# VectorE in the written order during part 1, and a longer lag for one head's first scores

## The chip, the cores and the metric

The kernel runs on one core of a Trainium2 chip. A core has five engines, each with its own instruction stream: TensorE (PE, matmuls), VectorE (DVE), ScalarE (ACT), GpSimd (POOL), and SyncE (SP), which issues most of the DMA transfers. The metric is the device time of one launch in microseconds, as the median of several runs. One launch runs one step of the whole layer.

## The reference

One layer of a streaming speech encoder, with 2048 prompt frames and 64 frames of a second stream ("sample") with a cache of 256 keys. Everything is float32. Cut to what matters here:

```python
h = rms_norm(x, norm1_g) * (1 + sc1) + sh1            # sc1, sh1, ... from silu(c) @ w_ada
z = h @ w_in
glu_a, glu_b, q, k, v, g_conv, g_attn = split(z)

u = glu_a * sigmoid(glu_b)                            # convolution branch, 512 channels
y = silu(layer_norm(depthwise_conv(u, width=31) + b)) @ w_conv_out

q, k = rms_norm(q), rms_norm(k)                       # attention branch, 8 heads of 64
s = q @ k.T * scale + rel_bias[head, clip(q_pos - k_pos)]
o = softmax(mask(s)) @ v                              # own chunk of 64 frames and the 8 before
attn_out = o @ w_attn_out

x = x + gt1 * ((sigmoid(g_conv) * y + sigmoid(g_attn) * attn_out) @ w_o)
gate, up = split((rms_norm(x, norm2_g) * (1 + sc2) + sh2) @ w_ffn_in)
x = x + gt2 * ((silu(gate) * up) @ w_ffn_out)
```

## The kernel before

To keep float32 accuracy at TensorE's faster rate, each operand is split into a high part and a low remainder (`hh` and `hl` for the input, `whi` and `wlo` for a weight, `ph` and `pl` for attention weights, `part_h` and `part_l` for what is stored). A product is three matmuls: high by high, low by high, high by low.

Part 1 makes everything up to the two branches' results. It takes the frames in four blocks (`PBLOCKS`, 576 rows and then three times 512), numbered 0 to 3. For each block the list `ORDER` names stages: the projections `q`, `k`, `v`, the four channel tiles of the convolution input, and the gates `g`. After a block's `v` its eight heads of attention are started; they run beside the block's convolution and gates and the next block's projections. In block 0 prompt heads alternate with the sample's heads, so the order of heads is (0,0), ("s",0), (0,1), ... ("s",7), then (1,0), (1,1) and so on. Part 2 reads the stored results back (`cin` is such a tile), merges the branches and runs the feed-forward part.

The code does not emit one step after the other. A planner (class `Stream`) counts the estimated load of each engine while instructions are written out. Work beside the projections is held in generators, sorted into lanes (`Lane`): norms, heads, convolution taps, the tail of the convolution. Every 500 ns of counted TensorE load a lane may advance by one step, if its due time has come and if VectorE or ScalarE isn't counted too full. A due time is the counted end of what the step needs, plus a constant. So the written order is already a schedule by the planner's count, not by the chip.

The instruction order on an engine is then made by a scheduler that may re-sort what was written; `tc.manual_schedule(engines=...)` turns that off for the engines listed, which then issue as written. In the kernel before this holds in part 1, after the first block's start (`first_block`), for TensorE alone (line 1642) until `ordered.close()`. VectorE, ScalarE, GpSimd and SyncE are re-sorted.

What a head does, in `attend` (from line 1509): `fetch` loads `q`, `kk` and a bias tile; after the due time in `loaded` the four score matmul groups (`sc`) follow one another, each as soon as VectorE has taken the row maximum (`pr`, `sm`) of one before it. ScalarE takes the exponent, VectorE the reciprocal of the sum. Then the weights are transposed (`ptp`), split into `ph` (ScalarE) and `pl` (VectorE) and multiplied by `vv` into `po`. `finish_head` divides, splits and stores the result (`o_p`, `part_h`, `part_l`).

The other names in the rows: `y<-u,wd,y` is one tap of the depthwise convolution on VectorE, `kn<-kn,r` a key or query norm that uses `r` from GpSimd, `ssq` and `t` its sums. `conv_norm` (from line 1294) is the tail of the convolution: normalise, then for each of four channel tiles a `y` and a `ln` step on VectorE, a split into `part_h` (ScalarE) and `part_l` (VectorE, `part_l<-ln`) and a store to `c_d`. The two tiles of `parts()` have `NS` = 2 buffers each, shared with all stores of part 1. `wmod` are weights of the modulation (`w_ada`), multiplied into `pa`. All compute instructions go through one helper, `Meter.run`, so nearly all rows of the profile carry its line, L105.

Of the kernel before, what the change touches and what calls it, by code (L numbers as in the profile page):

```python
# [622 lines left out]
def streaming_layer(ctx: ExitStack, tc: tile.TileContext, I, O):  # L623
# [481 lines left out]
    def cached_kv():  # L1105
        rows_ = [(src, j) for j in range(CACHE // P) for src in (ck, cv)]
        ts = []
        for i, (src, j) in enumerate(rows_):
            for src_, j_ in rows_[len(ts) : i + 2]:
                t = temp("cache")  # L1110
                nc.sync.dma_start(t, src_[j_ * P : (j_ + 1) * P])
                ts.append((t, stream.load["pe"] + CACHE_LAG))
            t, landed = ts[i]
            yield landed
            if src is ck:
                store_kq(t, P, k_d, j * P)
            else:
                store_v(t, P, j * P)
            yield
# [349 lines left out]
    def load_bias(h):  # L1469
        for r in (0, HD):  # L1470
            nc.sync.dma_start(
                bias[r : r + HD, HD - r : 640 - r],
                bass.AP(tensor=rb_d.tensor, offset=rb_d.offset + 768 * h + HD, ap=[[1, HD], [1, 576]]),
            )
        return bias

    ahead_qk, spare = {}, {"open": False, "heads": []}
    order, loaded, now = [], {}, {"scored": -1, "finished": -1, "bias": None}
# [8 lines left out]
    def fetch_qk(i):  # L1487
        if i < len(order) and ("qk", i) not in now:
            x, h = order[i]
            if spare["open"]:  # L1490
                spare["heads"].append(i)
            now["qk", i] = load_qk(x, h, *spans(x))

    def fetch(i):
        if i < len(order) and i not in loaded:
            x, h = order[i]
            fetch_qk(i)
            if now["bias"] is None or now["bias"][0] != h:
                now["bias"] = h, load_bias(h)
            first = x != "s" and (not i or order[i - 1][0] not in (x, "s"))  # L1500
            lag = FIRST_LAG if first else QK_LAG
            loaded[i] = max(stream.load["pe"] + BIAS_LAG, ahead_qk.get(i, stream.load["pe"] + lag))

# [5 lines left out]
    def attend(i):  # L1509
        x, h = order[i]  # L1510
        q0, nq, k0, nk = spans(x)
        yield lambda: now["scored"] == i - 1
        fetch(i)
        fetch_v(i)
        if not i:
# [7 lines left out]
        for t in range(0, nq, P):  # L1523
            n = min(P, nq - t)
            if x not in (0, "s"):
                ps = ps_a.tile([P, 2, 512], F32, tag="s", name="sc")
                for j in range(2):
                    for d in range(2):
                        pe.matmul(ps[:, j, :320], q2[:, d, t : t + P], kk[:, t + 320 * j : t + 320 * j + 320], start=d == 0, stop=d == 1)
                w, src, bs = 640, ps[:, :, :320], bias[:, ::-1]  # L1530
            else:
                w = nk if x == "s" else t + P

                if "banks" not in now:
                    sc = ps_a.tile([P, 2, 512], F32, tag="s", name="sc")
                    now["banks"] = [sc[:, 0:1], sc[:, 1:2]]
                ps = now["banks"].pop(0)
                now["banks"].append(ps)
                for d in range(2):
                    pe.matmul(ps[:n, 0, :w], q2[:, d, t : t + n], kk[:, :w], start=d == 0, stop=d == 1)  # L1540
                src, bs = ps[:n, 0:1, :w], bias[:n, 64:384][:, ::-1] if x == "s" else bias[:, :w][:, ::-1]
            pr, sm, free, ready = softmax_max(src, n, w, bs)
            tiles.append((pr, sm, n, w))
            if t + P < nq:
                yield free + PE_LAG, SCORE_ROOM
            else:
                fetch(i + 1)
                if (x, order[min(i + 2, len(order) - 1)][0]) in ((0, 0), ("s", "s")):
                    fetch_qk(i + 2)
                now["scored"] = i  # L1550
            if t:
                softmax_scale(*tiles[-2], x in ON_ACT)
# [86 lines left out]
    W = Weights((nc.sync, act, dve, gps), wpool, dram, stream, list(weight_order()), source, 3, 5, lambda key: key[0] in KEPT)  # L1639
    first_block(xs)  # L1640
    ordered = ExitStack()
    ordered.enter_context(tc.manual_schedule(engines={mybir.EngineType.PE}))
    norm_lane.add(cached_kv())
    mods = mod_steps()
    norms = {}
# [734 lines left out]
```

## Time and profile before

| | |
|---|---|
| median of 3 runs | 2958.93 us (2955.85 to 2965.5) |
| the profiled execution | 2957.35 us |
| its span in the trace | 2955.5 us |
| granted TensorE clock, mean | 0.995 |
| TensorE busy | 2892.0 us |
| VectorE busy | 2049.8 us |
| ScalarE busy | 1364.3 us |
| GpSimd busy | 1161.4 us |

The span is what the trace covers from the first to the last instruction; the time of the run has 1.85 us around it. A busy share is an average over the whole launch and says little about one stage, so the text reads rows of the stretch in question. In a row of the timeline the first two numbers are start and duration, and a bracket at the end gives the idle time of that engine just before it and what ended it. PEclk is the granted clock as a share of full speed.

### The profile page before, as it was taken

To read this page: it belongs to the slowest core of one execution; us is meant where nothing else is said; L and a number is where in the kernel's file an instruction comes from. 1 tells how busy PE (TensorE), PEld (TensorE's weight loads), DVE (VectorE), ACT (ScalarE), POOL (GpSimd) and SP (SyncE) were. 2 spreads that over 40 slices of the span, in tenths; PEclk is the share of its full clock that TensorE was granted. 3 is DMA by queue.
4 is the path that set the end of the run, shared out by engine and by line. 5 is a ranking of instruction groups with operands and counts; after the bars stand their busy time and mean duration, and the time that the engine had idled before them with its cause. 6 is when DMAs were issued, how large, how long until landed. Compare 5 with 4: busy or idle time off the path is not lost.

```text
span 2955.5 us, 44837 instructions
## 1 busy us (share of the span) xinstructions
PE 2892.0 (98%) x16193; PEld 2586.7 (88%) x16193; DVE 2049.8 (69%) x3648; ACT 1364.3 (46%) x2453; POOL 1161.4 (39%) x753
## 2 busy tenths in 40 slices
PE   7999999999999999999999999999999999999999
PEld 5899777887888788888999998999999999999998
DVE  5897787668857885477777756666666547566666
ACT  3345533661465267464334345444444345444442
POOL 1101210111011102454666452366667742465767
PEclk9999999999999999999999999999999999999999
DMA  9989899878996897985444876232333965333333
GB/s 320 312 297 309 274 283 324 269 229 294 285 313 209 294 264 239 290 298 171 147 147 143 268 257 227 93 120 91 114 122 104 331 225 185 97 99 108 115 106 126
DMA packets 467067, 628.04 MB, mean 212 GB/s; under 512 B 36196, under 2 KB 314584, under 8 KB 466845
## 3 DMA queue, kind: packets, MB, share of 16 engines
q1 hardware_dynamic: 452944, 606.11, 63.4%
q10 hardware_dynamic: 13901, 19.08, 1.9%
q8 instruction: 127, 2.08, 0.3%
q14 instruction: 95, 0.78, 0.1%
HBM read 476.53 MB, written 148.54 MB: 211 GB/s over the span
## 4 chain that ended last, share of the span: by engine, by line
PE 46%; DVE 2%; DMA 2%; ACT 1%; issue 1%; POOL 1%; SPq 0%; ACTq 0%; DVEq 0%; POOLq 0%
PE ps L105 28%; PE pd L105 13%; PE pw L105 5%; DVE wlo L105 1%; DMA cin<-o_d 1%; ACT whi L105 1%; POOL wlo L105 0%; DMA tg<-g_d 0%; DVE ps L105 0%; ACT xn L105 0%; DMA wst<-in_w_ffn_in 0%; DMA wfo<-in_w_ffn_out 0%; DVE acc L105 0%; DVE sums L105 0%; PE pt L105 0%
## 5 line engine op out<-in xcount | busy, mean ns | idle before, releaser
L105 PE MATMUL ps<-t,whi 128*128 128x384 f32 (+1 forms) x2112 | 501.9, 322 | 3.2 <-DVE u L105 1.1
L105 POOL TENSOR_TENSOR wlo<-wst,whi 128x1024 fp32r<-128x1024 f32 (+1 forms) x159 | 362.7, 2293 | 233.7 <-ACT whi L105 195.6
L105 ACT ACTIVATE whi<-wst 128x1024 fp32r<-128x1024 f32 (+1 forms) x265 | 258.2, 979 | 316.5 <-PE ps L105 127.1
L105 PE MATMUL ps<-b,whi 128*128 128x384 f32 (+1 forms) x1584 | 380.6, 325 | 5.4 <-DVE v L105 2.1
L105 PEld LDWEIGHTS ps<-t,whi 128*128 128x128 f32 x2112 | 367.8, 188 | 10.6 <-ACT u L105 3.1
L105 DVE SCALAR_TENSOR_TENSOR y<-u,wd,y 128x512 f32<-128x512 f32 (+1 forms) x480 | 370.1, 773 | 7.5
L105 PE MATMUL ps<-hh,whi 128*128 128x512 f32 (+2 forms) x992 | 363.4, 366 | 0.1
L105 DVE TENSOR_TENSOR acc<-acc,pd 128x512 f32<-128x512 f32 x482 | 322.3, 685 | 48.7 <-PE pd L105 46.0
L105 PE MATMUL ps<-hh,wlo 128*128 128x512 f32 (+2 forms) x992 | 345.6, 348 | 0.3 <-DVE wlo L105 0.3
L105 PE MATMUL ps<-hl,whi 128*128 128x512 f32 (+2 forms) x992 | 345.2, 348 | 0.0
L105 PE MATMUL ps<-t,wlo 128*128 128x384 f32 (+1 forms) x1056 | 338.2, 321 | 0.0
L105 PE MATMUL pd<-whi,hid 128*128 128x512 f32 x912 | 297.5, 391 | 0.3 <-DVE hid L105 0.3
L105 PEld LDWEIGHTS ps<-b,whi 128*128 128x128 f32 x1584 | 276.8, 188 | 13.6 <-DVE v L105 3.2
L105 ACT ACTIVATE pr<-pr,sm 128x640 f32<-128x640 f32 (+2 forms) x272 | 202.1, 749 | 153.9 <-DVE sm L105 150.9
L105 PE MATMUL ps<-b,wlo 128*128 128x384 f32 (+1 forms) x792 | 256.0, 323 | 0.0
L105 POOL TENSOR_TENSOR r<-t,mhalf 128x1 f32<-128x1 f32 (+2 forms) x68 | 82.4, 1219 | 414.8 <-DVE t L105 375.0
L105 PEld LDWEIGHTS ps<-hh,wlo 128*128 128x128 f32 x992 | 187.3, 189 | 23.3 <-DVE wlo L105 0.5
L105 DVE TENSOR_TENSOR wlo<-wst,whi 128x1024 fp32r<-128x1024 f32 (+1 forms) x106 | 135.7, 1284 | 99.2 <-ACT whi L105 98.2
L105 PEld LDWEIGHTS ps<-hh,whi 128*128 128x128 f32 x992 | 187.7, 189 | 18.0 <-issue 2.9
L105 PEld LDWEIGHTS pd<-whi,hid 128*128 128x128 f32 x912 | 171.1, 188 | 36.5 <-DVE acc L105 0.8
L105 PEld LDWEIGHTS ps<-hl,whi 128*128 128x128 f32 x992 | 188.1, 190 | 14.5 <-issue 1.7
L105 PEld LDWEIGHTS ps<-t,wlo 128*128 128x128 f32 x1056 | 198.0, 188 | 0.8
(233 smaller groups left out, 6299.1 us busy)
## 6 DMA issues: line engine op xcount, KB each, us to landing
whi<-w_din_h SPq DMA_DIRECT2D x72, 512.0 KB, 5.2
wlo<-w_din_l SPq DMA_DIRECT2D x72, 512.0 KB, 7.8
wst<-sum_d SPq DMA_DIRECT2D x131, 256.0 KB, 2.9
wfo<-in_w_ffn_out SPq DMA_DIRECT2D x64, 512.0 KB, 4.1
wmod<-in_w_ada SPq DMA_DIRECT2D x46, 512.0 KB, 9.1
sum_d<-ws SPq DMA_DIRECT2D x88, 256.0 KB, 2.2
wst<-in_w_ffn_in SPq DMA_DIRECT2D x85, 256.0 KB, 3.2
wst<-in_w_in SPq DMA_DIRECT2D x40, 512.0 KB, 7.2
```

Of the source, the lines that this page charges most:

```text
L105: self.last = f(*args, **kw)
```

## The change

Two lines change. On line 1642 VectorE is put on the list of engines that issue as written, beside TensorE. On line 1500 the condition for the longer lag changes. `FIRST_LAG` is 14000 and `QK_LAG` 9000, in nanoseconds of counted TensorE load. Before, the longer one held for a head that isn't the sample's and whose predecessor is neither of its own block nor the sample's: (0,0), (2,0) and (3,0). Now it holds for the first of all heads, and for a head of blocks 1 to 3 whose predecessor is of another block: (1,0) too, which follows ("s",7).

```diff
@@ -1497,7 +1497,7 @@
             fetch_qk(i)
             if now["bias"] is None or now["bias"][0] != h:
                 now["bias"] = h, load_bias(h)
-            first = x != "s" and (not i or order[i - 1][0] not in (x, "s"))
+            first = not i or x not in ("s", 0, order[i - 1][0])
             lag = FIRST_LAG if first else QK_LAG
             loaded[i] = max(stream.load["pe"] + BIAS_LAG, ahead_qk.get(i, stream.load["pe"] + lag))
@@ -1639,7 +1639,7 @@
     first_block(xs)
     ordered = ExitStack()
-    ordered.enter_context(tc.manual_schedule(engines={mybir.EngineType.PE}))
+    ordered.enter_context(tc.manual_schedule(engines={mybir.EngineType.PE, mybir.EngineType.DVE}))
     norm_lane.add(cached_kv())
```

The order of TensorE is the same before and after up to the first scores of head (1,0), but for one matmul that moves by a few rows in the first block, and again from the heads of block 2 on. The order of VectorE changes in most of part 1; from part 2 on it is the same.

The first place is VectorE near 355 us, at the end of block 0's `conv_norm`. Rows have operation, output, inputs and shape; a number behind a name tells one tile from the next. Before, the head's row maximum (`pr_4219`) comes after the first of the four `part_l<-ln` (4103), and of the later ones 4111 comes behind it:

```order
L105 TENSOR_SCALAR ln_4106<-ln_4106,y_776 128x512
L105 TENSOR_SCALAR y_776<-y_776,cols_175 128x512
L105 TENSOR_TENSOR part_l_4103<-ln_4098,part_h_4102 128x512
L105 TENSOR_SCALAR ln_4114<-ln_4114,y_776 128x512
L105 TENSOR_SCALAR y_776<-y_776,cols_175 128x512
L105 TENSOR_SCALAR ln_4122<-ln_4122,y_776 128x512
L105 TENSOR_TENSOR o32_p_4198<-other_4199,po_3906 64x512
L105 ISA pr_4219,sm_4220<-sc_1921,bias_194 128x128
L105 ISA sm_4220 128x1
L105 TENSOR_TENSOR part_l_4111<-ln_4106,part_h_4110 128x512
```

After, on the same engine, all four stand ahead of it (the first two are just above these rows), and so do another `part_l`, a `kn`, a reduction, `t` and `o_p`:

```order
L105 TENSOR_SCALAR ln_4114<-ln_4114,y_776 128x512
L105 TENSOR_TENSOR part_l_4119<-ln_4114,part_h_4118 128x512
L105 TENSOR_SCALAR y_776<-y_776,cols_175 128x512
L105 TENSOR_SCALAR ln_4122<-ln_4122,y_776 128x512
L105 TENSOR_TENSOR part_l_4127<-ln_4122,part_h_4126 128x512
L105 TENSOR_SCALAR part_l_4152<-pt_4146,gqk_179,part_h_4151 128x512
L105 TENSOR_TENSOR kn_4027<-kn_4027,r_4041 128x512
L105 TENSOR_REDUCE ssq_4094<-sq_4093 128x8
L105 TENSOR_SCALAR t_4165<-ssq_4094 128x8
L105 TENSOR_TENSOR o32_p_4198<-other_4199,po_3906 64x512
L105 ISA pr_4219,sm_4220<-sc_1921,bias_194 128x128
```

The maximum moved behind the whole tail of the convolution.

The second place is VectorE near 394 us, at the first maximum of the next prompt head (`pr_4559`), between taps of the convolution. Before:

```order
L105 TENSOR_SCALAR t_4553<-ssq_4527 128x8
L105 TENSOR_SCALAR y_4130<-u_4131,wd_178,y_4130 128x512
L105 TENSOR_TENSOR kn_4528<-kn_4528,r_4554 128x512
L105 TENSOR_SCALAR y_4130<-u_4131,wd_178,y_4130 128x512
L105 TENSOR_TENSOR part_l_4519<-o32_p_4198,part_h_4518 128x512
L105 TENSOR_SCALAR y_4130<-u_4131,wd_178,y_4130 128x512
L105 TENSOR_TENSOR pl_4576<-ptp_4574,ph_4575 128x128
L105 TENSOR_SCALAR part_l_4541<-pt_4535,gqk_179,part_h_4540 128x512
L105 TENSOR_SCALAR y_4130<-u_4131,wd_178,y_4130 128x512
L105 TENSOR_TENSOR pl_4576<-ptp_4574,ph_4575 64x64
L105 ISA pr_4559,sm_4560<-sc_1921,bias_194 128x128
```

After, on the same engine:

```order
L105 TENSOR_TENSOR part_l_4519<-o32_p_4198,part_h_4518 128x512
L105 TENSOR_TENSOR kn_4478<-kn_4478,r_4491 128x512
L105 TENSOR_SCALAR part_l_4541<-pt_4535,gqk_179,part_h_4540 128x512
L105 TENSOR_SCALAR y_4130<-u_4131,wd_178,y_4130 128x512
L105 TENSOR_REDUCE ssq_4527<-sq_4526 128x8
L105 TENSOR_SCALAR t_4553<-ssq_4527 128x8
L105 ISA pr_4559,sm_4560<-sc_1921,bias_194 128x128
L105 ISA sm_4560 128x1
L105 TENSOR_SCALAR y_4130<-u_4131,wd_178,y_4130 128x512
L105 TENSOR_TENSOR pl_4576<-ptp_4574,ph_4575 128x128
```

Here the maximum moved up: it passes the norm `kn_4528` and both `pl`.

The third place is TensorE near 480 us, between the modulation matmuls and the last scores of head (1,0) (`kk_5187`). Before, three rows of the projection lie between the two:

```order
L105 MATMUL pa_5375<-wmod_5258,cl_192 32x256 x4
L105 MATMUL ps_5394<-hh_195,whi_5107 128x512
L105 MATMUL ps_5394<-hl_196,whi_5107 128x512
L105 MATMUL ps_5394<-hh_195,wlo_5108 128x512
L105 MATMUL sc_5412<-kk_5187,q2_5186 128x320 x4
```

After, eighteen such rows and two more score groups lie between; the last of them:

```order
L105 MATMUL sc_5410<-kk_5187,q2_5186 128x320 x4
L105 MATMUL ps_5374<-hh_195,whi_5107 128x512
L105 MATMUL ps_5374<-hl_196,whi_5107 128x512
L105 MATMUL ps_5374<-hh_195,wlo_5108 128x512
L105 MATMUL pa_5355<-sel_193,R_5372 128x128 x2
L105 MATMUL ps_5374<-hh_195,whi_5161 128x512
L105 MATMUL ps_5374<-hl_196,whi_5161 128x512
L105 MATMUL ps_5374<-hh_195,wlo_5162 128x512
```

The head's scores moved down the projection's rows, and the `q` buffer that its last scores free comes free further down.

## The prediction

> **What bounds the kernel now.** I read the page first, then the waits and the busy time of the stretch that the change reaches, then the clock and the rows around the long waits.
>
> ```profile
> span 2955.5 us, 44837 instructions
> PE 2892.0 (98%) x16193; PEld 2586.7 (88%) x16193; DVE 2049.8 (69%) x3648; ACT 1364.3 (46%) x2453; POOL 1161.4 (39%) x753
> PE 46%; DVE 2%; DMA 2%; ACT 1%; issue 1%; POOL 1%; SPq 0%; ACTq 0%; DVEq 0%; POOLq 0%
> ```
>
> TensorE (PE) is busy for 98% of the span. The edits remove no matmul, so they can only change how long PE waits and how fast its clock runs. The given order of VectorE (DVE) ends with part 1; part 2 begins with the matmuls that read `cin` (the last row below), at 1180.8 us. So the stretch to judge is 100 to 1190 us:
>
> ```profile
> 100.00:1190.00 1090.00, 1061.83 (x6035) 908.30 (x6033) 830.66 (x1591) 538.81 (x1027) 146.28 (x129) 0.99 0.86 278
> 100.00:200.00 100.00, 98.11 (x620) 88.89 (x619) 93.38 (x140) 37.22 (x61) 12.24 (x11) 1.00 0.88 306
> ...
> PE sc L105 <- DVE sm L105: 11.7, 8, 5.7
> PE sc L105 <- DMA kk<-k_d: 4.6, 2, 4.3
> PE pt L105 <- DVE u L105: 1.9, 1, 1.9
> ...
> 1180.79 0.80 PE L105 MATMUL ps<-cin,whi 128*128 128x320 f32 x2 [1.40 <-DVE o_p L105]
> ```
>
> The first two rows give length, then busy PE, weight loads, DVE, ACT and POOL, then the granted clock, the DMA share and GB/s. PE stands idle 1090 − 1061.8 = 28.2 us, which is the ceiling of a gain by waits. The largest item is score matmuls (`sc`) that wait for a row maximum (`sm`) on DVE, 11.7 us in 8 waits; then one load of keys (`kk`). DVE itself is 76% busy, but 93% from 100 to 200 us.
>
> A long wait costs a second time, by the clock behind it (the number after POOL's bracket):
>
> ```profile
> 309.00:316.00 7.00, 6.69 (x36) 6.56 (x37) 4.28 (x16) 5.78 (x16) 2.96 (x3) 0.76 0.86 287
> 395.00:404.00 9.00, 8.98 (x30) 7.62 (x31) 6.83 (x16) 4.32 (x13) 0.21 (x1) 0.57 0.99 359
> 495.00:498.00 3.00, 3.00 (x9) 2.61 (x10) 0.00 (x0) 0.00 (x0) 0.00 (x0) 0.50 0.52 130
> ...
> 309.31 0.50 PE L105 MATMUL sc<-kk,q 128*128 128x256 f32 x2 [2.86 <-DVE sm L105]
> 357.57 0.51 PE L105 MATMUL sc<-kk,q 128*128 128x256 f32 x2 [0.92 <-DVE sm L105]
> 395.01 0.79 PE L105 MATMUL sc<-kk,q 128*128 128x256 f32 x2 [5.70 <-DVE sm L105]
> 495.00 1.40 PE L105 MATMUL sc<-kk,q 128*128 128x320 f32 x4 [4.29 <-DMA kk<-k_d]
> ```
>
> Behind the three waits of 2.86, 5.70 and 4.29 us the clock is 0.76, 0.57 and 0.50. Lost that way: 7 × 0.24 = 1.7 us, 9 × 0.43 = 3.9 us and 3 × 0.50 = 1.5 us.
>
> **The lag of head (1,0).** The planner holds this head's first scores back by a longer count of PE time. Summing the spacing of the PE rows that now stand ahead (24 of 128x512, 0.235 us each), its first scores come 5.6 us later, its last 3.9 us later, the next head's first scores 3.9 us later. The modulation matmuls (`pa<-wmod`) have two score groups less ahead of them, so they come 1.4 us earlier.
>
> ```profile
> 476.98 0.64 PE L105 MATMUL pa<-wmod,cl 128*32 128x256 f32 x8 [0.59 <-DMA wmod<-in_w_ada]
> 478.35 0.64 PE L105 MATMUL pa<-wmod,cl 128*32 128x256 f32 x8 [0.73 <-DMA wmod<-in_w_ada]
> ...
> 477.00 3.15 SPq L249 DMA_DIRECT2D wmod<-in_w_ada  x4
> 481.06 0.60 SPq L1427 DMA_DIRECT2D q<-q_d  x1
> ...
> wmod<-in_w_ada SPq DMA_DIRECT2D x46, 512.0 KB, 9.1
> ```
>
> `wmod` already arrives late, by 0.59 + 0.73 = 1.3 us, and its loads don't move: that wait grows to 2.7 us. With `pa` pinned by its data, the shifts behind it become 3.9 + 1.4 = 5.3 us. The loads of the next head need the `q` buffer that this head's last scores free, so they go out near 486.4 instead of 481.06, and are wanted near 496.0 instead of 495.0 − 4.29 = 490.7. The room stays 9.6 us; before, it took 13.9 us from the first issue to the end of the wait. But four `wmod` loads of 512 KB stand ahead in the same queue, issued until 480.2 and landing 9.1 us later at the median, so near 489; the new loads go out at the end of that and not in its middle: 13.9 − 5.3 = 8.6 us fits. I take the 4.29 us and the 1.5 us of clock as gone, 1.4 us as paid to `wmod`, and half of a 1.5 us clock fall for its longer wait: −4.29 − 1.5 + 1.4 + 0.8 = −3.6 us. Ends: −5.8 (no new wait at all) and +2.9 (the load as late as ever, `wmod` with its clock fall on top).
>
> By the Trainium skill, TensorE: Matmul & The Clock Gate, section "What's actually happening", the clock falls after an idle window of about 3.4 us. Here it fell after 2.86 us already (the 0.76 above), so the row decides; by the page the three short `wmod` waits would not lower it, and the term would be −4.4 us.
>
> **DVE in given order, from 340 to 395 us.** This is the end of block 0's convolution branch beside its attention.
>
> ```profile
> PE sc L105 <- DVE sm L105: 7.0, 3, 5.7
> PE ps L105 <- DVE hl L105: 1.3, 1, 1.3
> PE ps L105 <- DVE part_l L105: 0.7, 1, 0.7
> ...
> 354.25 0.68 DVE L105 TENSOR_TENSOR part_l<-ln,part_h 128x512 fp32r<-128x512 f32 x1
> 357.24 0.28 DVE L105 CUSTOM_DVE_ANT_0 pr<-sc,bias 128x128 f32<-128x128 f32 x1
> 390.37 0.69 DVE L105 TENSOR_TENSOR kn<-kn,r 128x512 f32<-128x512 f32 x1 [1.53 <-POOL r L105]
> 394.68 0.27 DVE L105 CUSTOM_DVE_ANT_0 pr<-sc,bias 128x128 f32<-128x128 f32 x1
> ...
> L1348 SPq DMA_DIRECT2D c_d<-part_l x4: 319/320/320, 355.0 to 365.4; - x4
> DMA to landing us min/median/max: 2.0/3.0/4.5
> ```
>
> The three wait rows are those of 340 to 396 us: 9.0 us of idle PE. Before, the maximum at 357.24 passes three of the four `part_l<-ln`. Now it stands behind all four, one more `part_l`, a `kn`, a reduction, `t` and `o_p`. `part_h` and `part_l` have two buffers, so the third and fourth pair wait for the store of the pair two before. The first `part_l` ends at 354.9, its store goes out at 355.0 and lands 2.0 to 3.0 us later; the second pair follows about 1.3 us behind; so the fourth `part_l` can end near 360.5. Behind it lie 0.74 + 0.69 + 0.68 + 0.2 + 0.67 = 3.0 us. The maximum comes near 363.5 instead of 357.2: a new PE wait of 6.3 us, and behind it a clock fall of 1.5 to 3.9 us.
>
> But the next limit is the maximum at 394.68, 37.4 us later, and between the two DVE is hardly idle. The given order takes out of this stretch the three `part_l<-ln` and the `part_l` (4 × 0.7 = 2.8 us), puts in a `kn` (0.7), and lets the second maximum pass a `kn` with its 1.53 us of waiting and two `pl` (0.69 + 0.5). That leaves 37.4 − 2.8 + 0.7 − 1.2 − 1.5 = 32.6 us: near 396, or 394 where the other short waits in it close too. So PE's idle time moves from 395 to 357 and mostly stays the same; what goes is the slow clock behind 395, what comes is a slow clock at 357 inside time that was idle. Between −4.3 us (all of the second slow stretch saved, and the maximum 0.4 earlier) and +9 (6.3 + 2.7, if nothing is taken back at 395). I take −2 us, nearer the first, since the DVE rows between are full.
>
> **At 305 us** the same thing happens small:
>
> ```profile
> 304.08 0.28 DVE L105 TENSOR_TENSOR pl<-ptp,ph 128x128 fp32r<-128x128 f32 x1
> 305.71 0.21 DVE L105 TENSOR_TENSOR part_l<-ln,part_h 128x64 fp32r<-128x64 f32 x1
> 308.96 0.29 DVE L105 CUSTOM_DVE_ANT_0 pr<-sc,bias 128x128 f32<-128x128 f32 x1 [0.65 <-DMA bias<-rb_d]
> ```
>
> The narrow `part_l<-ln` now stands ahead of `pl`, which then leaves later than 304.08; PE stops at the `po` that reads it, about 1.3 us before it stops now, and the maximum at 308.96 waits for its bias load as before. +1.3 us; ends 0 and +3.
>
> **Elsewhere.**
>
> ```profile
> 570.01 0.85 PE L105 MATMUL sc<-kk,q 128*128 128x320 f32 x4 [0.81 <-DVE sm L105]
> 987.12 0.27 PE L105 MATMUL pt<-ident,u 128*30 128x128 f32 x1 [1.92 <-DVE u L105]
> ...
> 179.10 0.27 DVE L105 CUSTOM_DVE_ANT_0 pr<-sc,bias 128x128 f32<-128x128 f32 x1
> ...
> DVE pl L105 <- ACT ph L105: 44.4, 61, 4.4
> DVE kn L105 <- POOL r L105: 31.7, 22, 3.9
> ```
>
> In both the awaited operation moves ahead of a tap of the convolution, each about 0.8 us long: −1.6 us together; ends −2.7 (both waits gone) and 0. The two fills of `bias` and the `rr` table move behind the first norms; their first user is the maximum at 179.10, far behind, so nothing. SP's stores and loads and ACT's steps are re-sorted around these places; the buffers they wait for are the ones counted above. The convolution tails of blocks 1 to 3 have attention work written between their slices in the given order, so I count no second burst.
>
> The sum: −3.6 − 2 + 1.3 − 1.6 = −5.9 us. The profiled execution took 2957.35 us, 1.6 us under the median of 2958.93, so 2951.4 by its own time and 2953 against the median.
>
> **Rivals.** *Faster:* the given order keeps the maxima on time everywhere. What speaks for it: the 11.7 us are all head starts or band maxima passed by work that could wait. Then 11.7 us and the clock falls of 1.7 and 3.9 go besides the 3.6: −20.9 us, 2938. Against it: the bias load and the store waits above are no matter of order.
>
> *Slower:* a waiting DVE instruction now holds everything behind it. Before, other work filled the 44.4 us and 31.7 us of waits above only in part; from 100 to 200 us DVE has 6.6 us to spare in 100. If the 6.3 us and 2.7 us of block 0 are not taken back at 395, and each of the three other tails pays 6.3 us, it is 9 + 18.9 + 1.3 − 3.6 − 1.6 = +24 us, 2983. It decides from about 15 us of new waits on (8.9 for a loss that shows, and the 5.9 gained), that is from block 0 and one more tail. The Trainium skill, PSUM — Partial Sum Buffer, section "Engine vs sequencer instructions", says that VectorE's queue is strictly first in, first out; it is the rule behind this rival. No row of the run before can show its price, since that order was another.
>
> *Nothing:* the key load again takes 13.9 us and the wait merely moves with the scores, while the other terms cancel to within a microsecond or two: 2957 to 2960. That two of the shifts are equal speaks for it, the drained queue against it.
>
> **Chances.** The forecast 0.40, with its own range of 2944 to 2965 from the ends above; the faster rival 0.28; the slower 0.25; nothing 0.07. A measurement of this kernel can tell about 0.3%, 8.9 us, from no change. The forecast lies 3 us inside that on the fast side, so 0.10 of its 0.40 counts as faster, 0.27 as the same and 0.03 as slower: faster 0.38, same 0.34, slower 0.28. The range for 8 in 10 takes in the fast rival and most of the slow one: 2935 to 2981.
>
> **What the profile after would show.** The wait of `sc` for `kk` at 495 gone and the clock there at 1.0; the `wmod` wait near 2.7 us; a wait of some 6 us at 357 and none over 2 at 395; `u` at 985 near 1.1 us. I am wrong if DVE's waits for ACT or POOL turn up as PE waits in the tails of blocks 1 to 3 (slower), or if PE's idle time from 100 to 1190 us falls under 15 us (faster).

## The result and the profile after

The changed kernel takes 2973.45 us (median of 6 runs, 2971.17 to 2979.39), the kernel before 2958.11 us (6 runs, 2954.56 to 2965.5). The ratio is 1.0048, with a 95% interval of 1.0038 to 1.0059: about 14 us slower. The forecast was 2953 us, 6 us faster.

The page of the changed kernel shows nearly the same work in a longer span:

```profile
span 2969.6 us, 44908 instructions
PE 2895.6 (98%) x16193; PEld 2586.6 (87%) x16193; DVE 2049.4 (69%) x3648; ACT 1361.9 (46%) x2453; POOL 1162.4 (39%) x753
```

TensorE is busy 3.6 us longer with the same 16193 matmuls, so that is slower clock and not more work (the mean granted clock is 0.994 for 0.995); the other 10.5 of the 14.1 us are new idle time. The waits of TensorE from 100 to 1190 us (total, times, longest) name it; the last row is from the kernel before:

```profile
PE sc L105 <- DVE sm L105: 18.7, 12, 8.1
PE ptp L105 <- ACT pr L105: 6.5, 8, 1.3
PE po L105 <- DVE pl L105: 2.2, 1, 2.2
PE pa L105 <- DMA wmod<-in_w_ada: 2.1, 3, 0.7
PE ps L105 <- DVE wlo L105: 2.0, 2, 1.4
...
PE ptp L105 <- ACT pr L105: 0.7, 2, 0.5
```

The wait for `kk`, 4.6 us before, is gone. But score matmuls wait 18.7 us for row maxima (11.7 before), transposes 6.5 us for ScalarE's scaled weights, which come after VectorE's reciprocals (0.7 before), and VectorE's weight splits are late too.

The order of TensorE is the same in both up to 466 us, but for a few rows near 62 us, and again from 754 us on, so the same matmul can be followed in both traces. The lag of the changed kernel behind the kernel before, at a few of them:

| matmul, before | before, us | after, us | behind, us | its stretch added |
|---|---|---|---|---|
| `pa<-wmod` in the first block | 49.8 | 50.1 | 0.3 | +0.3 |
| `ptp` of the first prompt head | 194.1 | 203.6 | 9.5 | +9.2 |
| `hl` products at 341.7 | 341.7 | 350.8 | 9.1 | −0.4 |
| first `sc` of the prompt head after | 395.0 | 409.9 | 14.9 | +5.8 |
| `sc` of a later head of block 0 | 436.2 | 452.6 | 16.4 | +1.5 |
| second scores of block 2 | 757.2 | 768.1 | 10.9 | −5.5 |
| first `cin` of part 2 | 1180.8 | 1197.0 | 16.2 | +5.3 |

Part 2, where all orders are the same, gives 2 us back. So there are three losses, up to 204 us, from 341 to 410, and in blocks 2 and 3, and one gain between 452 and 768 us, where head (1,0) and the rest of block 1 lie.

**Up to 204 us.** First VectorE in the kernel before:

```profile
85.83 2.62 DVE L105 SCALAR_TENSOR_TENSOR y<-u,wd,y 128x606 f32<-128x606 f32 x3
90.78 0.75 DVE L105 SCALAR_TENSOR_TENSOR part_l<-pt,gqk,part_h 128x512 fp32r<-128x512 f32 x1 [1.67 <-ACT part_h L105]
153.20 1.22 DVE L105 TENSOR_TENSOR wlo<-wst,whi 128x1024 fp32r<-128x1024 f32 x1
155.09 1.22 DVE L105 TENSOR_TENSOR wlo<-wst,whi 128x1024 fp32r<-128x1024 f32 x1
156.99 1.22 DVE L105 TENSOR_TENSOR wlo<-wst,whi 128x1024 fp32r<-128x1024 f32 x1
```

Rows of VectorE, then ScalarE, SyncE and TensorE, of the changed kernel:

```profile
91.06 0.75 DVE L105 SCALAR_TENSOR_TENSOR part_l<-pt,gqk,part_h 128x512 fp32r<-128x512 f32 x1 [4.64 <-DMA q_d<-part_l]
161.48 3.49 DVE L105 TENSOR_TENSOR wlo<-wst,whi 128x1024 fp32r<-128x1024 f32 x3
169.23 1.22 DVE L105 TENSOR_TENSOR wlo<-wst,whi 128x1024 fp32r<-128x1024 f32 x1 [3.65 <-ACT whi L105]
...
168.13 1.06 ACT L105 ACTIVATE whi<-wst 128x1024 fp32r<-128x1024 f32 x1 [6.56 <-DMA wst<-in_w_in]
...
162.73 0.38 SPq L384 DMA_DIRECT2D wst<-in_w_in  x1
...
186.04 0.50 PE L105 MATMUL sc<-kk,q 128*128 128x256 f32 x2 [2.68 <-DVE sm L105]
203.64 0.33 PE L105 MATMUL ptp<-ident,pr 128*128 128x128 f32 x1 [1.29 <-ACT pr L105]
```

At 91 us a `part_l` waits 4.64 us for a store, and the taps that filled this time before now stand behind it. At 161 us three `wlo` stand behind seven taps; only then do their `wst` buffers come free, the next load goes out at 162.7, ScalarE gets it at 168.1, and VectorE itself waits 3.65 us for that. The maximum behind all this starts at 185.69 us, where it started at 179.10 before, and TensorE waits 2.68 us. VectorE is 93% busy there, which would leave it little time to catch up. This chain is read from the rows; that the given order causes the loss is tested below (e8), the chain and the part of the load in it are not isolated.

**From 341 to 410 us.** VectorE:

```profile
355.87 0.55 DVE L105 TENSOR_SCALAR y<-y,cols 128x512 f32<-128x512 f32 x1 [3.45 <-ACT ln L105]
362.04 0.69 DVE L105 TENSOR_TENSOR part_l<-ln,part_h 128x512 fp32r<-128x512 f32 x1 [2.33 <-ACT part_h L105]
365.67 0.69 DVE L105 TENSOR_TENSOR part_l<-ln,part_h 128x512 fp32r<-128x512 f32 x1 [1.75 <-ACT part_h L105]
370.82 0.75 DVE L105 SCALAR_TENSOR_TENSOR part_l<-pt,gqk,part_h 128x512 fp32r<-128x512 f32 x1 [1.84 <-DMA c_d<-part_l]
373.48 0.28 DVE L105 CUSTOM_DVE_ANT_0 pr<-sc,bias 128x128 f32<-128x128 f32 x1
379.41 0.42 DVE L105 COPY R<-pa 128x256 f32<-128x256 f32 x1 [1.67 <-PE pa L105]
...
364.85 0.28 ACT L105 ACTIVATE ph<-ptp 128x128 fp32r<-128x128 f32 x1 [2.84 <-PE ptp L105]
365.02 0.62 ACT L105 ACTIVATE part_h<-ln 128x512 fp32r<-128x512 f32 x1
...
373.81 0.80 PE L105 MATMUL sc<-kk,q 128*128 128x256 f32 x2 [8.10 <-DVE sm L105]
409.93 0.79 PE L105 MATMUL sc<-kk,q 128*128 128x256 f32 x2 [2.83 <-DVE sm L105]
```

The four slices of the tail went one by one, as forecast, but not for the stores alone: VectorE waits 3.45 us for `ln` and then for `part_h`, both on ScalarE. The third `part_h` stands on ScalarE behind a `ph` that waits 2.84 us for TensorE, and TensorE soon waits for VectorE. The new wait is 8.1 us where 6.3 + 0.9 was forecast. And the clock (behind POOL's bracket) fell behind both waits, at 373 and again at 409, where the forecast had it saved:

```profile
373.00:382.00 9.00, 8.19 (x55) 5.48 (x55) 4.46 (x14) 3.00 (x9) 1.85 (x2) 0.70 0.87 285
409.00:418.00 9.00, 8.07 (x29) 6.90 (x30) 7.83 (x20) 3.15 (x10) 1.85 (x2) 0.62 0.96 367
186.00:193.00 7.00, 6.96 (x40) 6.96 (x41) 6.86 (x11) 2.18 (x6) 0.00 (x0) 0.76 1.05 396
```

### The profile page after: what moved, and what is told of

Its sections match the earlier page's. It is cut to its first block, busy times and chain, and to the rows that moved or that the text cites. A ratio compares the mean times of both kernels' runs of the same rounds, so it can differ in the third digit from the quotient of the medians.

```text
span 2969.6 us, 44908 instructions
## 1 busy us (share of the span) xinstructions
PE 2895.6 (98%) x16193; PEld 2586.6 (87%) x16193; DVE 2049.4 (69%) x3648; ACT 1361.9 (46%) x2453; POOL 1162.4 (39%) x753
## 4 chain that ended last, share of the span: by engine, by line
PE 47%; DVE 2%; DMA 1%; ACT 1%; issue 1%; POOL 0%; SPq 0%; ACTq 0%; DVEq 0%
PE ps L105 28%; PE pd L105 13%; PE pw L105 5%; DVE wlo L105 1%; ACT whi L105 0%; DVE ps L105 0%; DMA cin<-o_d 0%; DMA x<-x_d 0%; DMA wst<-in_w_conv_out 0%; DMA wfo<-in_w_ffn_out 0%; ACT xn L105 0%; DVE sums L105 0%; DMA tg<-g_d 0%; PE pt L105 0%; ACT t L105 0%
## 5 line engine op out<-in xcount | busy, mean ns | idle before, releaser
L105 DVE SCALAR_TENSOR_TENSOR y<-u,wd,y 128x512 f32<-128x512 f32 (+1 forms) x480 | 373.2, 778 | 11.3
L105 ACT ACTIVATE pr<-pr,sm 128x640 f32<-128x640 f32 (+2 forms) x272 | 198.5, 747 | 145.9 <-DVE sm L105 142.8
```

The source lines that it names most:

```text
L105: self.last = f(*args, **kw)
```

## The experiments

The theory after the result: the given order of VectorE loses in several places, because an instruction that waits there holds row maxima and weight splits behind it; the lag gives a few microseconds back. The rivals: the lag itself costs; the loss is made in one place and only travels; stores alone hold VectorE. Ratios are against the kernel before, run beside each. "Given" is VectorE in written order, "sorted" by the scheduler. The kernel before was run again beside each group of runs, with medians of 2958.63, 2960.9 and 2959.37 us, so the ratios compare better than the medians.

| run | VectorE given | lag | else | median, us | ratio (95%) |
|---|---|---|---|---|---|
| changed kernel | all of part 1 | longer | | 2973.45 | 1.0048 (1.0038 to 1.0059) |
| e1_dve_only | all of part 1 | as before | | 2974.94 | 1.0052 (1.0038 to 1.0066) |
| e2_lag_only | sorted | longer | | 2954.67 | 0.9984 (0.9975 to 0.9992) |
| e3_from_b1 | from 420 us | longer | | 2960.75 | 1.0001 (0.9992 to 1.0009) |
| e8_from_g0 | from 180 us | longer | | 2966.87 | 1.0024 (1.0016 to 1.0033) |
| e4_b0_only | up to 420 us | longer | | 2964.62 | 1.0009 (1.0000 to 1.0018) |
| e10_act_too | all, ScalarE too | longer | | 3010.98 | 1.0163 (1.0148 to 1.0179) |
| e5_ns3 | all of part 1 | longer | 3 part buffers | 2971.44 | 1.0032 (1.0020 to 1.0044) |
| e7_nt5 | all of part 1 | longer | control of e5 | 2975.89 | 1.0047 (1.0030 to 1.0064) |
| e11_pool_given | all of part 1 | longer | 12 `wlo` on GpSimd | 2995.26 | 1.0122 (1.0108 to 1.0136) |
| e12_pool_sorted | sorted | longer | 12 `wlo` on GpSimd | 2974.08 | 1.0047 (1.0034 to 1.0059) |
| e13_lag_ns3 | sorted | longer | 3 part buffers | 2953.84 | 0.9978 (0.9969 to 0.9987) |

### The two edits apart

Only the given order (the changed kernel with the old lag):

```diff
-            first = not i or x not in ("s", 0, order[i - 1][0])
+            first = x != "s" and (not i or order[i - 1][0] not in (x, "s"))
```

> Only VectorE's given order, the lag as before. Theory (the given order costs about 16 us up to head (1,0), because a waiting VectorE instruction holds the row maxima behind it; the lag gives back the key load's wait): slower than the changed kernel by the 4.3 us wait and its slow clock, so 2976 to 2980 us, with the wait of sc for kk back near 4 us. Rival (the lag is what costs): 2958 to 2965.

Only the lag (the changed kernel with VectorE sorted):

```diff
-    ordered.enter_context(tc.manual_schedule(engines={mybir.EngineType.PE, mybir.EngineType.DVE}))
+    ordered.enter_context(tc.manual_schedule(engines={mybir.EngineType.PE}))
```

> Only the longer lag for head (1,0); VectorE sorted by the scheduler. Theory: the 4.3 us wait for kk and the slow clock behind it go, the wmod wait grows by at most 1.4 us: 2952 to 2956 us. Rival (the wait moves with the scores): 2957 to 2960; rival (the lag costs): above 2962.

The lag alone makes the kernel faster, 0.9984; its 2954.67 us lie in what the theory expected. The given order alone makes it slower, 1.0052. So the rival that the lag costs has fallen. In the given order the lag is worth less, 1.5 us between the two medians, which is not clear of the noise: there the wait for `kk` with the shorter lag is 2.0 us and not 4.3. That fits e1 coming out just under its 2976 us.

In the run with the lag alone the `wmod` matmuls show what the forecast had priced; the last row is the same place in e3 (below), with the same lag:

```profile
477.71 0.64 PE L105 MATMUL pa<-wmod,cl 128*32 128x256 f32 x8 [0.47 <-DMA wmod<-in_w_ada]
479.06 0.64 PE L105 MATMUL pa<-wmod,cl 128*32 128x256 f32 x8 [0.71 <-DMA wmod<-in_w_ada]
480.44 0.64 PE L105 MATMUL pa<-wmod,cl 128*32 128x256 f32 x8 [0.73 <-DMA wmod<-in_w_ada]
...
480.00:484.00 4.00, 3.56 (x23) 2.75 (x24) 1.83 (x4) 0.54 (x1) 0.00 (x0) 1.00 1.02 413
...
480.00:483.00 3.00, 3.00 (x14) 2.53 (x11) 0.81 (x2) 0.00 (x0) 0.12 (x1) 0.64 1.02 408
```

Their wait is 1.9 us in three pieces, where 1.3 us stood before and 2.7 us were forecast, and the clock behind them stays at 1.00. No wait for `kk` appears. But the clock does not always stay up here: in e3, behind `wmod` waits of 0.62, 0.69 and 0.73 us, it is 0.64, and in e13, behind four of 0.49 to 0.70 us, 0.52 from 477 to 484 us.

### Where the given order loses

The lag alone, and on top of it VectorE given from a later point on:

```diff
     for b, stage in ORDER:
         lo, hi = PBLOCKS[b]
+        if (b, stage) == (1, 2):
+            ordered.enter_context(tc.manual_schedule(engines={mybir.EngineType.DVE}))
```

> Longer lag, and VectorE in given order only from stage (1, 2) on, near 420 us, so that block 0 with its convolution tail stays sorted. Theory (the loss is made in block 0, in the first 205 us and at 357): about 16 us less than the changed kernel, 2955 to 2959 us. Rival (the given order loses a little everywhere, or the three later tails pay as well): 2964 to 2972.

The same with `(0, "g")` in place of `(1, 2)`:

> Longer lag, and VectorE in given order from stage (0, g) on, near 180 us: the first 200 us stay sorted, block 0's convolution tail is in given order. Theory: the 9.5 us lost by 204 us come back, the 6 us at 357 to 395 stay: 2962 to 2967 us, with a wait of sc for sm of some 6 to 8 us near 360. Rival (the wait at 357 is only the echo of the late start): under 2960.

From the lag alone over e3 and e8 to the changed kernel the ratio climbs from 0.9984 to 1.0001, 1.0024 and 1.0048: +5.0 us for the given order from 420 us on, +6.8 us for 180 to 420 us, +7.1 us for what lies before 180 us (each difference of ratios by 2958 us; the medians, 6.1, 6.1 and 6.6 us, show that such a step is good to a microsecond or two). e8 lies within its expectation; e3 is just above, and the 5.0 us say that the later blocks pay as well, where the theory had them at nothing. The first `sc` behind block 0's tail in e8 and in e3:

```profile
367.19 0.80 PE L105 MATMUL sc<-kk,q 128*128 128x256 f32 x2 [6.18 <-DVE sm L105]
```

```profile
358.61 0.51 PE L105 MATMUL sc<-kk,q 128*128 128x256 f32 x2 [0.92 <-DVE sm L105]
```

With the start sorted, e8 still waits 6.18 us; with the tail sorted too, the wait is 0.92 us as before. So that loss is no echo of the late start. In the later blocks no single wait is long. In the changed kernel they are of this size:

```profile
772.70 0.64 PE L105 MATMUL pa<-wmod,cl 128*32 128x256 f32 x8 [0.72 <-DMA wmod<-in_w_ada]
807.50 0.33 PE L105 MATMUL ptp<-ident,pr 128*128 128x128 f32 x1 [0.79 <-ACT pr L105]
1058.44 0.33 PE L105 MATMUL ptp<-ident,pr 128*128 128x128 f32 x1 [1.08 <-ACT pr L105]
```

The other half, again on top of the lag alone, given up to 420 us and sorted from there:

```diff
+    early = ExitStack()
+    early.enter_context(tc.manual_schedule(engines={mybir.EngineType.DVE}))
...
+        if (b, stage) == (1, 2):
+            early.close()
```

> Longer lag, VectorE in given order up to stage (1, 2) near 420 us only. If the stretches add up (changed kernel 2973.5 less the 6.1 us that the run with given order from stage (1, 2) lay above the lag alone): 2965 to 2969 us. If they interact: outside of that.

The median of 2964.62 us is just under the interval; by the ratio beside it, 1.0009, it is 7.4 us above the lag alone, where the two stretches of block 0 were 6.8 + 7.1 = 13.9 us in the other series. So by the times the stretches do not add up: the later blocks alone cost 5.0 us and block 0 alone 7.4, both together 18.9.

The traces narrow down where. TensorE's order is the same in these kernels but for a few rows near 64 us, so the first `cin` of part 2 can be compared. It starts at 1176.57 us with the lag alone, at 1185.87 in e3, 1187.90 in e4 and 1196.95 us in the changed kernel. That is 9.3, 11.3 and 20.4 us behind the lag alone, and there the two halves do add up. In e4 the lag is 9.0 us at 500 us and 9.6 us at 1050 us, so a sorted VectorE makes up nothing in blocks 1 to 3. By the end of the spans e4 is 6.4 us behind, e3 6.8 and the changed kernel 16.9. So what is made up is made up in part 2, where VectorE is sorted in all of them: 4.9, 2.5 and 3.5 us. Why the amounts differ is not shown, and there is one trace of each.

### What holds VectorE at 357 us

ScalarE is sorted in the changed kernel, while VectorE is not. Its order there, in rows from operation to shape, with three steps of other work (`tb`, `other`, `ph`) among the tail's:

```
L105 ACTIVATE part_h_4102<-ln_4098 128x512
L105 ACTIVATE ln_4122<-y_776,lnh_177 128x512
L105 ACTIVATE tb_4183<-ps_4133 128x512
L105 ACTIVATE other_4199<-po_3906 64x512
L105 ACTIVATE part_h_4110<-ln_4106 128x512
L105 ACTIVATE ph_4228<-ptp_4227 128x128
L105 ACTIVATE part_h_4118<-ln_4114 128x512
L105 ACTIVATE part_h_4126<-ln_4122 128x512
```

Two runs are to tell ScalarE's order from the stores. ScalarE in written order too:

```diff
-    ordered.enter_context(tc.manual_schedule(engines={mybir.EngineType.PE, mybir.EngineType.DVE}))
+    ordered.enter_context(tc.manual_schedule(engines={mybir.EngineType.PE, mybir.EngineType.DVE, mybir.EngineType.Activation}))
```

> The changed kernel with ScalarE in written order too; VectorE's order is the same. Theory (near 357 VectorE in written order waits for part_h on ScalarE, which the scheduler put behind steps that wait for TensorE): VectorE's waits for part_h there shrink, the wait of sc for sm falls from 8.1 us to 3 to 5 us, and the time is 2963 to 2970 us unless ScalarE's own waits cost more elsewhere. Rival (stores of the two part buffers are what holds VectorE): the wait near 357 stays 7 to 9 us.

Three part buffers, with its control:

```diff
-    NT, NS = 7, 2
+    NT, NS = 5, 3
```

> The changed kernel with three instead of two part_h and part_l buffers; to make room the pool of temporaries has five instead of seven. TensorE's and VectorE's order is the same. Theory of the stores (the prediction's): the wait of 4.6 us for q_d at 91 us and most of the 8.1 us at 357 go, 2964 to 2969 us. Rival (VectorE waits for ScalarE, not for stores): the wait at 357 shrinks by 2 us at most, and the time is 2969 to 2975.

```diff
-    NT, NS = 7, 2
+    NT, NS = 5, 2
```

> Control for the run with three part buffers: the changed kernel with five temporaries and two part buffers. If the temporaries do not matter: 2971 to 2976 us, as the changed kernel.

The waits of VectorE from 340 to 385 us, in the changed kernel, then with three part buffers, then with ScalarE given:

```profile
DVE part_l L105 <- ACT part_h L105: 7.1, 5, 2.3
DVE y L105 <- ACT ln L105: 3.5, 1, 3.5
DVE part_l L105 <- DMA c_d<-part_l: 1.8, 1, 1.8
```

```profile
DVE part_l L105 <- ACT part_h L105: 4.5, 5, 1.6
DVE y L105 <- ACT ln L105: 3.5, 1, 3.5
```

```profile
DVE y L105 <- ACT ln L105: 4.9, 1, 4.9
DVE part_l L105 <- ACT part_h L105: 2.9, 4, 0.7
DVE part_l L105 <- DMA c_d<-part_l: 1.0, 1, 1.0
```

And the wait of the first `sc` behind them with three part buffers, 8.1 us in the changed kernel:

```profile
369.91 0.80 PE L105 MATMUL sc<-kk,q 128*128 128x256 f32 x2 [3.69 <-DVE sm L105]
```

With three buffers the wait falls by 4.4 us, to 3.69, and the median lies 4.4 us under its control. So the store round trip was worth about half of this wait, more than the rival allowed and less than the store theory wanted; the time, 2971.44 us, lies in the rival's range. The control shows that the temporaries change nothing here (2975.89 us, 1.0047). At 91 us the store theory missed: with three buffers VectorE still waits there, 5.32 us up to 91.44 us. What is left is VectorE standing for `ln` and then 0.7 us in each slice for `part_h`, one after the other, with the maximum behind.

ScalarE in written order cuts the waits for `part_h` from 7.1 to 2.9 us, as expected, but the wait of `sc` only from 8.1 to 6.5 us, because `ln` comes later; and over all it costs 34 us more than the changed kernel (1.0163 against 1.0048). Its rows of waits, ScalarE from 100 to 1190 us and TensorE from 100 to 1230 us, show part of why: ScalarE now stands longer, and TensorE waits longer for maxima.

```profile
ACT pr L105 <- DVE sm L105: 276.4, 150, 10.2
...
PE sc L105 <- DVE sm L105: 28.8, 30, 6.5
```

In the changed kernel they were 142.8 us (111 times) and 18.7 us (12 times). The rest of the 34 us was not taken apart. So the written order on ScalarE is no remedy: it lowers the wait at the tail by 1.6 us and makes the rest worse. Since it moves ScalarE's steps everywhere, this run does not show what ScalarE's order at the tail alone is worth.

### Does VectorE's load decide up to 205 us?

Twelve of the weight splits (171 on GpSimd where there were 159; the expectations counted 11) moved from VectorE to GpSimd, in the changed kernel and in the one with the lag alone:

```diff
-        on_dve = key[0] == "in" or key[0] == "qkv" and (passing or key[1]) or turn % 2
+        on_dve = key[0] == "in" and i % 2 or key[0] == "qkv" and (passing or key[1]) or turn % 2
```

> The changed kernel with 11 of VectorE's weight splits (wlo, 1.2 us each, most of them from 100 to 200 us) moved to GpSimd. Theory (up to 205 us the given order loses because VectorE, 93% busy there, cannot catch up after a wait): 3 to 7 us less than the changed kernel, 2967 to 2971 us, with the wait of sc for sm near 186 us under 1 us. Rival (the loss there does not hang on how full VectorE is): within 2 us of the changed kernel.

> Control: the same move of 11 weight splits in the kernel with the longer lag alone, VectorE sorted. Theory: sorted, VectorE's fullness costs little, so within 2 us of the lag alone, 2953 to 2958 us. Rival (GpSimd relieves both alike): 2948 to 2952.

Both miss by some 20 us, the control too, so these runs do not answer the question, and it stays open: the move costs by itself, and with the work counted on another engine TensorE's written order is another too, up to 682 us. Taps and splits from 105 to 210 us (count, busy, mean ns) in e11, and last the taps of the changed kernel:

```profile
L105 DVE SCALAR_TENSOR_TENSOR y<-u,wd,y 128x606 f32<-128x606 f32 x74 | 71.1, 961 | 1.8
L105 POOL TENSOR_TENSOR wlo<-wst,whi 128x1024 fp32r<-128x1024 f32 x5 | 13.0, 2607 | 28.0 <-ACT whi L105 28.0
L105 DVE TENSOR_TENSOR wlo<-wst,whi 128x1024 fp32r<-128x1024 f32 x9 | 10.9, 1225 | 0.8 <-ACT whi L105 0.8
...
L105 DVE SCALAR_TENSOR_TENSOR y<-u,wd,y 128x606 f32<-128x606 f32 x73 | 61.9, 848 | 1.7
```

In the changed kernel the same taps took 848 ns each. VectorE was not relieved: 74 taps at 113 ns more are 8.4 us, about what the splits that left this stretch (9 for 16) had cost it (7 × 1.2 us). What remains is that the given order costs about the same here, 21.2 us between e11 and e12, as 18.8 us between the changed kernel and the lag alone.

### The lag with three part buffers

The edit of e5 on the kernel with the lag alone:

> The longer lag alone with three part buffers and five temporaries. If stores held VectorE only in the given order: within 2 us of the lag alone, 2953 to 2957 us. If they also cost in sorted order: 2948 to 2952.

Sorted, the third buffer is worth at most 2 us (2953.84 against 2954.67 us; 0.9978 against 0.9984, intervals that overlap), against 4.4 us in the given order. So it is mainly in the given order that the stores matter. This is the fastest version measured, if by less than the noise: 0.9978 of the kernel before (0.9969 to 0.9987).

## Why the prediction was wrong, and where it was right

The step that failed is the sum's silence on what VectorE's own lateness does: it has no term for the start of the given order, which cost 9.2 us, and none for blocks 2 and 3, which cost 5.3 us. And it lets the new wait at 357 be paid back at 395: the two together were to gain 2 us and lost 5.8. Term by term:

- **The lag of head (1,0), −3.6 us.** Right. Alone it measured 0.9984, which is −4.7 us; the wait for `kk` and the slow clock behind it went, and the rival "nothing" fell. The `wmod` wait grew to 1.9 and not 2.7 us. In e2 the clock did not fall behind it (1.00 from 480 to 484 us), as the rule of the Trainium skill (TensorE: Matmul & The Clock Gate, section "What's actually happening") would have it; in e3 and e13, with much the same waits, it did fall (0.64 and 0.52). So half a clock fall was a fair price.
- **340 to 395 us, −2 us.** Wrong, +5.8 us. The new wait at 357 was foreseen with its place and nearly its size (6.3 more forecast, 7.2 more measured), but the size is in part luck: it was reckoned from stores alone, and three buffers took only 4.4 of the 8.1 us away; the rest is VectorE waiting for ScalarE's `ln` and `part_h`, which the working leaves out. The step that failed is "the next limit is the maximum at 394.68", by which I let PE's idle time only move. VectorE's stretch between the two maxima took 36.1 us and not 32.6. Of the 3.5 us, some 2.4 are idle time of VectorE, above all for `pa` and `part_h`, which were late through TensorE itself (1.67 and 1.6 us), and 1.2 are work that the forecast did not count there. So 2.8 us of wait were left at 395, and a second slow clock stood behind them.
- **305 us, +1.3 us.** The mechanism at `po` was right, it waits 2.17 us for `pl`; but the maximum's wait of 2.86 us behind it, which the forecast kept, closed entirely, and from 281 to 309 us (times of before) the stretch came out 0.5 us shorter.
- **Elsewhere, −1.6 us.** The waits at 570 and 987 us shrank as forecast (0.81 to none, 1.92 to 1.22 us). But the sum had no term at all for the start of the given order, +9.2 us up to 204 us, and none for blocks 2 and 3, +5.3 us. Of the start the working names only the fills of `bias` and the `rr` table, and puts them at nothing because their first user, the maximum at 179.10, is far behind; that maximum came 6.6 us later, and the clock fell behind the wait for it. For the start I laid the traced times of the other engines along the new order and found VectorE on time; its own lateness, which frees `wst` late and so delays the loads it waits for next, is not in those times. For the later blocks I looked for one burst in the convolution tails and found none. The loss is made of waits of 0.4 to 1.1 us for `pr`, `sm` and `wmod`.
- **The slower rival** had the mechanism, an instruction that waits holds everything behind it, and named the stretch with 6.6 us to spare. Its price was set in the wrong places, the three later tails, and at 2983 us it was too dear. The Trainium skill's strict order of VectorE's queue (PSUM — Partial Sum Buffer, "Engine vs sequencer instructions") agrees with the long waits here: 4.64 us at 91 and 3.65 us at 169, with taps standing behind whose input was there, and 3.45 us at 356, with the tail and the next head's maximum behind.
- **The faster rival** fell: the waits for maxima rose to 18.7 us.
- **The range** of 2935 to 2981 held 2973.45, and slower had 0.28. The forecast's own range, 2944 to 2965, did not hold it. It was to come "from the ends above", but those add up to −12.8 and +14.9 us, which is 2946 to 2974. That this wider range just holds the result is luck: the 9.2 and 5.3 us are in none of its ends.

## What to carry to other kernels

An order that is written by a planner's count has only the planner's durations in it; putting one more engine into that order takes away the scheduler's habit of letting ready work pass a waiting step, and beside one long wait the loss here came in many small ones that no single place shows. When an order changes on one engine, do not lay the old times of the other engines along it: ask which loads and buffers that engine itself releases, and follow them once around. Judge the two halves of a kernel at the same matmul and not by total times alone, since a later part can take some of a loss back. Where two edits come together, time each alone first; here one was worth 4 to 5 us and the other cost 19.

## What was not expected of the hardware

- In the runs that moved weight splits from VectorE to GpSimd, VectorE's taps were longer, 848 to 961 ns each (843 to 948 ns in sorted order), beside GpSimd steps of 2.6 us. The Trainium skill, SBUF — State Buffer, section "SBUF: two separate sides", says that VectorE steps with two inputs from this memory and GpSimd steps lock a shared port pair against each other. The longer taps agree with that; no run here isolates it.
- The clock fell to 0.62 over 9 us behind a wait of 2.83 us (at 409) and to 0.76 over 7 us behind one of 2.68 us (at 186). Behind shorter waits the same place came out both ways: three of 0.5 to 0.7 us within 4 us left it at 1.00 in e2 and came before 0.64 in e3; the wait of 1.9 us for `u` near 985 us left it at 1.00 in the kernel before (986 to 990 us) and came before 0.61 with the lag alone (981 to 985 us). So in these traces the length of a wait alone does not tell whether the clock falls.
